# A hybrid SSD and Fourier block: dt cut into steps between gate products, and the order of the last projection pairs

## The chip, the cores and the metric

One NeuronCore of a Trainium2 chip runs the whole program. The metric is the time of one execution on the device, in microseconds (us); the median of several executions counts. All times of the trace are us from the start of the span.

## What is computed

One layer: an input projection of 1024 latent tokens and 256 context tokens, a bidirectional state-space scan (SSD) beside a Fourier mixer, gates, an output projection and a SwiGLU FFN. The part that the change touches is the step size dt of the scan and what is made of it, and the projection columns around it:

```python
u = h @ w_in[i]                                     # x, B, C, dt, z, fft, gate columns
uc = hc @ w_in[i][:, :SSD_IN_WIDTH]
xbc = jax.nn.silu(dwconv_centred(u[..., :CONV_DIM], conv_w, conv_b))
dt_l = jax.nn.softplus(dtr[:, :, d] + bias)
a = -jnp.exp(a_log[d])
a_cum = jnp.cumsum((dt * a), axis=2)                # within chunks of 128
decay_to_end = jnp.exp(a_cum[:, :, -1:] - a_cum)
chunk_decay = jnp.exp(a_cum[:, :, -1])
lmat = decay_matrix(a_cum)                          # exp of differences, lower triangle
y_off = jnp.einsum('bclgn,bcgjpn,bclgj->bclgjp', cc, entering, jnp.exp(a_cum))
gates = jax.nn.sigmoid(u_gate)
```

## The kernel before

All matrices are float32, held as a high and a low part (`hi`, `lo`), so that a product is three matmuls. In the projection stage two blocks of 128 columns are made together by `pair`: it splits two weight tiles and forms seven products p1 to p7 of 512 x 512 (a Strassen-like scheme), each of 12 matmuls, with the input's sums `hT1` to `hT4` prepared beforehand; `combine` (lines 566 to 576) adds them into two padded rows `pads[0]` and `pads[1]`. The order of the products is p1, p2, p4, p6, p3, p7, p5 (another one for the first pair). Behind each product but the first, `trs()` takes one entry of the list `tr` and runs it.

`block_pair(b)` is a pair of x, B or C columns. Its `emit` runs `a_conv` on both pads: a copy with scale on ScalarE (line 429), four multiply-adds on VectorE (line 432), Silu (line 434), and a store for B and C. The result lies in a tile named `cv`, of which there are two in turn. Up to b = 24 its list `tr` transposes the two blocks before. `gate_pair(j)` is a pair of gate columns: `combine`, tanh in the pads (line 683) and a store to `s_gate` from the pads. In what follows x22 is `block_pair(22)` and g0 is `gate_pair(0)`.

The list `steps` is x2 to x22, then g0, x24, g2, x26, g4, x28, g6, x30, g8. `dt_product` has made the raw dt earlier and left it in `s_dt`. After step 14 (x26) `phase_dt` runs whole: it loads dT into a `cv` tile, turns it by ten transposes (line 614) and keeps u and e in a second `cv` tile; softplus is a reciprocal and a polynomial (lines 621 to 633); two matmuls with triangles cumulate (line 641), two more pick the chunk ends (line 646), ScalarE makes `decp` by 18 small exponentials (line 651) and `ea_all`; eight transposes and 16 writes bring the cumulated rows to `s_a` from a third `cv` tile `ar` (line 663); a fourth, `dc`, serves the logarithm (lines 670 to 675). At the end a loop restores `hB12` from `s_q` (lines 718 to 721), whose place hT4 had taken.

PSUM in this stage: pool `ppm` has three banks, pool `ppa` two banks `tr` and three banks `mm`. `a_ps` counts its calls in `nmm` and takes a bank of `ppa` where the count is odd, of `ppm` where it is even. The scan stage behind it takes the banks of `ppm` for its fill products (`fill_ps`) and those of `ppa` for states and outputs; its fill starts with z columns, whose results `zs` lie where the pads were. `NGP = 5` gate pairs are made in the projection stage, the gate blocks 10 to 14 in the scan stage.

In this stage no order is written out by hand. The program gives the instructions in an order, and a scheduler with a timing model lays them on each engine's queue as their inputs become ready in its model. On the chip each engine runs its queue in order.

Of the kernel before, what the change touches and what calls it, by code (L numbers as in the profile page):

```python
# [9 lines left out]
F32 = mybir.dt.float32  # L10
F32R = mybir.dt.float32r
AF = mybir.ActivationFunctionType
ALU = mybir.AluOpType
# [128 lines left out]
def _build(nc, tc, h, o, hook, stop, es):  # L142
# [357 lines left out]
    def pair(src, tr, ctx, emit, late=False):  # L500
# [102 lines left out]
        nc.scalar.copy(out=dT[:, 1024:1280], in_=pss[2][:64, :LC])  # L603
        nc.sync.dma_start(out=s_dt, in_=dT[:, :1280])

    def phase_dt():
        dT = pa.tile([P, 1282], F32, name="cv", bufs=2)[:64]
        nc.sync.dma_start(out=dT[:, :1280], in_=s_dt)
        ue = pa.tile([P, 1282], F32, name="cv", bufs=2)
        u = ue[:, :640].rearrange("p (a b) -> p a b", b=64)  # L610
        for q0 in (0, 5):
# [5 lines left out]
        uf = u.rearrange("p a b -> p (a b)")  # L617
        e = ue[:, 640:1280]
        r = pq = a_all.rearrange("p a b -> p (a b)")
        acc = wst_all.rearrange("p a b -> p (a b)")  # L620
        nc.vector.scalar_tensor_tensor(out=e, in0=uf, scalar=-1.0, in1=uf, op0=ALU.mult, op1=ALU.min)
        nc.scalar.activation(out=e, in_=e, func=AF.Exp)
        nc.vector.tensor_scalar(out=r, in0=e, scalar1=2.0, scalar2=None, op0=ALU.add)
        nc.vector.reciprocal(out=r, in_=r)
        nc.vector.scalar_tensor_tensor(out=e, in0=e, scalar=2.0, in1=r, op0=ALU.mult, op1=ALU.mult)
        nc.vector.tensor_tensor(out=pq, in0=e, in1=e, op=ALU.mult)
        cf = [1.0 / ((2 * k + 1) * 4.0 ** k) for k in range(9)]
        nc.vector.tensor_scalar(out=acc, in0=pq, scalar1=cf[8], scalar2=None, op0=ALU.mult)
        for k in range(7, 0, -1):
            nc.vector.scalar_tensor_tensor(out=acc, in0=acc, scalar=cf[k], in1=pq, op0=ALU.add, op1=ALU.mult)  # L630
        nc.vector.scalar_tensor_tensor(out=acc, in0=acc, scalar=1.0, in1=e, op0=ALU.add, op1=ALU.mult)
        dtf = dt_all.rearrange("p a b -> p (a b)")
        nc.vector.scalar_tensor_tensor(out=dtf, in0=uf, scalar=0.0, in1=acc, op0=ALU.max, op1=ALU.add)
        ae = rows[:, 64:128]
        nc.scalar.activation(out=ae, in_=ae, func=AF.Exp)
        da = e.rearrange("p (a b) -> p a b", b=64)
        nc.vector.scalar_tensor_tensor(out=da, in0=dt_all, scalar=-1.0, in1=ae[:, None, :].to_broadcast([P, NTA, 64]),
                                       op0=ALU.mult, op1=ALU.mult)
        for d, tri in ((0, tri_f), (1, tri_b)):
            ps = ppa.tile([P, 512], F32, name="tr", bufs=2)  # L640
            nc.tensor.matmul(ps[:, :320], lhsT=tri, rhs=da[:, :, 32 * d:32 * d + 32], start=True, stop=True)
            nc.scalar.copy(out=a_all[:, :, 32 * d:32 * d + 32], in_=ps[:, :320].rearrange("p (a b) -> p a b", b=32))
        ex = acc.rearrange("p (a b) -> p a b", b=64)
        for d, sel in ((0, e127), (1, e0)):
            ps = ppa.tile([P, 512], F32, name="tr", bufs=2)
            nc.tensor.matmul(ps[:, :320], lhsT=sel, rhs=a_all[:, :, 32 * d:32 * d + 32], start=True, stop=True)
            psv = ps[:, :320].rearrange("p (a b) -> p a b", b=32)
            nc.vector.tensor_tensor(out=ex[:, :, 32 * d:32 * d + 32], in0=psv, in1=a_all[:, :, 32 * d:32 * d + 32], op=ALU.subtract)
            order = [8, 9, 0, 1, 2, 3, 4, 5, 6] if d == 0 else [9, 8, 7, 6, 5, 4, 3, 2, 1]
            for i, c_ in enumerate(order):  # L650
                nc.scalar.activation(out=decp[:, i, d, :], in_=psv[:, c_, :], func=AF.Exp)
        nc.scalar.activation(out=ex, in_=ex, func=AF.Exp)
        nc.vector.tensor_tensor(out=wst_all, in0=dt_all, in1=ex, op=ALU.mult)
        nc.scalar.activation(out=ea_all, in_=a_all[:, :NT, :], func=AF.Exp)
        ar = pa.tile([P, 1282], F32, name="cv", bufs=2)[:64, :1024].rearrange("p (a b) -> p a b", b=P)
        for q0 in (0, 4):
# [4 lines left out]
        for d in range(2):  # L661
            for g in range(NG):
                nc.sync.dma_start(out=s_a[g, :, d].rearrange("c j l -> j c l"),
                                  in_=ar[32 * d + 4 * g:32 * d + 4 * g + 4])


        lg, cl = u[:, :NT, :], dt_all[:, :NT, :]
        el = e[:, :NT * 64].rearrange("p (a b) -> p a b", b=64)
        dc = pa.tile([P, 1282], F32, name="cv", bufs=2)[:, :NT * 64].rearrange("p (a b) -> p a b", b=64)
        nc.vector.tensor_scalar(out=dc, in0=cl, scalar1=1.2e-38, scalar2=None, op0=ALU.max)  # L670
        nc.scalar.activation(out=lg, in_=dc, func=AF.Ln)
        nc.scalar.activation(out=el, in_=lg, func=AF.Exp, scale=-1.0)
        nc.vector.tensor_tensor(out=el, in0=el, in1=dc, op=ALU.mult)
        nc.vector.scalar_tensor_tensor(out=lg, in0=el, scalar=-1.0, in1=lg, op0=ALU.add, op1=ALU.add)
        nc.vector.tensor_tensor(out=a_all[:, :NT, :], in0=lg, in1=a_all[:, :NT, :], op=ALU.subtract)
        nc.vector.tensor_tensor(out=tri_b, in0=tri_b, in1=ident, op=ALU.subtract)

    def gate_pair(j):
# [38 lines left out]
    for i in range(4):  # L717
        for q in range(2):
            t = small()
            nc.sync.dma_start(out=t, in_=s_q[2 * i + q])  # L720
            nc.vector.tensor_copy(out=hB12[i][q], in_=t)
    hstack_t.close()
    phA.close()
    if hook is not None:
        for nm, t in (("dt_all", dt_all), ("a_all", a_all), ("wst_all", wst_all), ("ea_all", ea_all), ("decp", decp)):
            hook(nm, t)
    if stop == "A":
        right.close(); hstack.close()
# [931 lines left out]
```

## Time and profile before

| | us |
|---|---|
| median of 3 runs | 2282.3 |
| lowest and highest | 2280.68, 2285.83 |
| the profiled execution | 2281.2 |
| its span, first to last instruction | 2279.4 |
| TensorE busy in the span | 2165.9 (95%) |
| VectorE busy | 1627.0 (71%) |
| ScalarE busy | 991.4 (43%) |
| GpSimd busy | 741.8 (33%) |

The page of the profile gives busy time per engine, the span in 40 slices, and the costliest groups of instructions. PE is TensorE, PEld its weight loads, DVE VectorE, ACT ScalarE, POOL GpSimd, SP the engine that issues the transfers. A view by stretches gives busy time of each engine between two times, the count of records in brackets, and the granted TensorE clock as a share of 2.4 GHz. A timeline gives start, duration, engine, line, operation and tiles of each instruction, and in square brackets the idle time before it with what ended it. A list of waits adds up who waited for whom.

### The profile page before, as it was taken

To read this page: it belongs to the slowest core of one execution; us is meant where nothing else is said; L and a number is where in the kernel's file an instruction comes from. 1 tells how busy PE (TensorE), PEld (TensorE's weight loads), DVE (VectorE), ACT (ScalarE), POOL (GpSimd) and SP (SyncE) were. 2 spreads that over 40 slices of the span, in tenths; PEclk is the share of its full clock that TensorE was granted. 3 is DMA by queue.
4 is the path that set the end of the run, shared out by engine and by line. 5 is a ranking of instruction groups with operands and counts; after the bars stand their busy time and mean duration, and the time that the engine had idled before them with its cause. 6 is when DMAs were issued, how large, how long until landed. Compare 5 with 4: busy or idle time off the path is not lost. (4 is left out here: it accounts for less than half of the span.)

```text
span 2279.4 us, 32757 instructions
## 1 busy us (share of the span) xinstructions
PE 2165.9 (95%) x11560; PEld 1813.0 (80%) x11560; DVE 1627.0 (71%) x2783; ACT 991.4 (43%) x2094; POOL 741.8 (33%) x610
## 2 busy tenths in 40 slices
PE   7999999999689999999999999999798999999997
PEld 1778888886588999999989887777576888887876
DVE  5878888888657777877736558826987566775678
ACT  4444444433345666767743212124422332334443
POOL 1532111110125555555521222135343333332222
PEclk9999999999799999999999999999899999999999
DMA  8122223432254555555454546551486224457755
GB/s 289 64 73 88 83 84 130 143 119 93 90 171 152 176 160 171 173 175 178 156 188 164 177 159 245 186 187 65 127 276 226 92 98 162 166 177 242 237 194 185
DMA packets 167101, 360.28 MB, mean 158 GB/s; under 512 B 17548, under 2 KB 57228, under 8 KB 166296
## 3 DMA queue, kind: packets, MB, share of 16 engines
q1 hardware_dynamic: 166936, 358.18, 47.0%
q8 instruction: 91, 1.49, 0.3%
q14 instruction: 74, 0.61, 0.1%
HBM read 267.34 MB, written 90.78 MB: 157 GB/s over the span
## 5 line engine op out<-in xcount | busy, mean ns | idle before, releaser
L199 POOL TENSOR_TENSOR wlo<-wraw,whi 128x1024 fp32r<-128x1024 f32 (+1 forms) x83 | 201.5, 2431 | 634.3 <-ACT whi L198 631.5
L198 ACT CAST whi<-wraw 128x1024 fp32r<-128x1024 f32 (+1 forms) x123 | 126.8, 1036 | 237.6 <-PE dm L210 84.2
L203 PE MATMUL fill<-whi,hhi 128*128 128x256 f32 x768 | 223.1, 292 | 7.1 <-DVE pad L576 5.8
L432 DVE SCALAR_TENSOR_TENSOR cv<-pad,vecs,cv 128x1282 f32<-128x1282 f32 (+1 forms) x128 | 213.8, 1709 | 7.8 <-ACT cv L429 7.4
L204 PE MATMUL fill<-wlo,hhi 128*128 128x256 f32 x768 | 218.1, 284 | 0.0
L205 PE MATMUL fill<-whi,hlo 128*128 128x256 f32 x768 | 217.4, 284 | 0.0
L874 ACT ACTIVATE abc<-abc,a_all 128x128 f32<-128x128 f32 x512 | 158.2, 392 | 88.4 <-DMA abc<-s_a 84.1
L203 PE MATMUL fp<-m,oph 128*128 128x512 f32 x452 | 181.3, 402 | 14.0 <-ACT oph L1343 10.4
L205 PE MATMUL fp<-m,opl 128*128 128x512 f32 x452 | 181.7, 403 | 8.0 <-DVE opl L1344 5.0
L204 PE MATMUL fp<-m,oph 128*128 128x512 f32 x452 | 181.2, 401 | 0.0
L495 PE MATMUL mm<-tq,whi 128*128 128x512 f32 x480 | 153.8, 401 | 1.4 <-ACT whi L198 1.4
L203 PEld LDWEIGHTS fill<-whi,hhi 128*128 128x128 f32 x768 | 145.8, 190 | 9.4 <-issue 6.2
L495 PE MATMUL mm<-hhi,whi 128*128 128x512 f32 x320 | 127.7, 400 | 22.4 <-DVE pad L570 22.4
L204 PEld LDWEIGHTS fill<-wlo,hhi 128*128 128x128 f32 x768 | 146.3, 191 | 0.7
L205 PEld LDWEIGHTS fill<-whi,hlo 128*128 128x128 f32 x768 | 146.0, 190 | 0.5
L495 PE MATMUL mm<-hlo,whi 128*128 128x512 f32 x320 | 127.1, 397 | 0.0
L495 PE MATMUL mm<-hhi,wlo 128*128 128x512 f32 x320 | 126.9, 397 | 0.0
L203 PEld LDWEIGHTS fp<-m,oph 128*128 128x128 f32 x452 | 86.5, 191 | 36.1 <-ACT oph L1343 11.7
L205 PEld LDWEIGHTS fp<-m,opl 128*128 128x128 f32 x452 | 86.3, 191 | 32.0 <-DVE opl L1344 7.6
L495 PEld LDWEIGHTS mm<-tq,whi 128*128 128x128 f32 x480 | 89.7, 189 | 22.7 <-ACT whi L198 2.5
L850 DVE SCALAR_TENSOR_TENSOR S<-S,decp,st 128x64 f32<-128x64 f32 x512 | 105.0, 273 | 0.0
L876 DVE COPY_PREDICATED abc<-misc,abc 128x512 f32<-128x512 int32 x64 | 52.3, 818 | 71.2 <-ACT abc L874 71.1
(408 smaller groups left out, 5919.0 us busy)
## 6 DMA issues: line engine op xcount, KB each, us to landing
abc<-s_a SPq DMA_DIRECT2D x64, 512.0 KB
fraw<-in_wfi SPq DMA_DIRECT2D x44, 512.0 KB
wraw<-in_wxbc SPq DMA_DIRECT2D x32, 512.0 KB
dx<-in_wada SPq DMA_DIRECT2D x32, 512.0 KB
wraw<-in_wzf SPq DMA_DIRECT2D x24, 512.0 KB
gt<-s_gate SPq DMA_DIRECT2D x24, 512.0 KB
fi<-in_wfo SPq DMA_DIRECT2D x22, 512.0 KB
s_cw<-fo SPq DMA_DIRECT2D x44, 256.0 KB
```

Of the source, the lines that this page charges most:

```text
L198: nc.scalar.copy(out=hi[:, :cols], in_=raw[:, :cols])
L199: (eng or nc.gpsimd).tensor_tensor(out=lo[:, :cols], in0=raw[:, :cols], in1=hi[:, :cols].bitcast(F32), op=ALU.subtract)
L203: nc.tensor.matmul(ps, lhsT=a[0], rhs=b[0], start=start, stop=False)
L204: nc.tensor.matmul(ps, lhsT=a[0], rhs=b[1], start=False, stop=False)
L205: nc.tensor.matmul(ps, lhsT=a[1], rhs=b[0], start=False, stop=stop)
L432: nc.vector.scalar_tensor_tensor(out=v[:, :n], in0=pd[:, t:t + n], scalar=cwh[:, 5 * b + t:5 * b + t + 1], in1=v[:, :n], op0=ALU.mult, op1 ...
L495: nc.tensor.matmul(ps, lhsT=lhs[x], rhs=b[i][y], start=i == 0 and (x, y) == (0, 0), stop=i == 3 and (x, y) == (1, 0))
L850: nc.vector.scalar_tensor_tensor(out=sn[:, hd_], in0=S[-1][:, hd_], scalar=decp[:, i, d, 4 * g + j:4 * g + j + 1], in1=sv_[:, hd_], op0=AL ...
L874: nc.scalar.activation(out=abc[:, d, j, :], in_=abc[:, d, j, :], func=AF.Identity, scale=-1.0, bias=a_all[:, c, hd:hd + 1])
L876: nc.vector.copy_predicated(out=E, mask=tri_b.bitcast(mybir.dt.int32)[:, None, :].to_broadcast([P, HPG, P]), data=abc[:, 1])
```

## The change

It does three things. `phase_dt` becomes `dt_steps`, which returns lists of short functions; each list is given to a gate pair as its `tr` list, so that `trs()` runs one function behind each product but the first. g0 gets the load, the transposes and the softplus down to the first polynomial steps, g2 the rest of it, the cumulation, the exponentials and the writes of `s_a`, g4 the logarithm; g6 gets nothing, and g8 gets the four restores of `hB12` behind two empty functions. The tiles change: u lies in `dt_all`, e in the tile that later holds `ea_all` and `decp`; a `cv` tile serves dT, one serves `ar`, and two serve the logarithm. Each gate pair now stands behind its x pair: x22, x24, g0, x26, g2, x28, g4, x30, g6, g8. And before g8 the count `nmm` is made even, so its p1 takes a bank of `ppa`, p2 one of `ppm`, and so on. The 18 exponentials into `decp` become three. The gate blocks of the scan stage stay.

```diff
-    NGP, DTP = 5, 14
+    NGP = 5
...
-    ea_all = dpool.tile([P, NT, 64], F32, name="ea_all")
-    decp = dpool.tile([P, 9, 2, 32], F32, name="decp")
+    ead = dpool.tile([P, NT * 64 + 9 * 64], F32, name="ead")
+    ea_all = ead[:, :NT * 64].rearrange("p (a b) -> p a b", b=64)
+    decp = ead[:, NT * 64:].rearrange("p (a b c) -> p a b c", b=2, c=32)
...
         def trs(n=1):
             for _ in range(n):
                 if tr:
-                    a_transposes(*tr.pop(0))
+                    f = tr.pop(0)
+                    f() if callable(f) else a_transposes(*f)
...
-    def phase_dt():
+    def dt_steps():
+        u = dt_all
+        e = ead[:, :640]
+        r = pq = a_all.rearrange("p a b -> p (a b)")
+        acc = wst_all.rearrange("p a b -> p (a b)")
...
+        def load():
+            dT = keep["dT"] = pa.tile([P, 1282], F32, name="cv", bufs=2)[:64]
+            nc.sync.dma_start(out=dT[:, :1280], in_=s_dt)
+            nc.scalar.activation(out=ae, in_=ae, func=AF.Exp)
+
+        def turn(q0):
+            tp = ppa.tile([P, 512], F32, name="tr", bufs=2)
...
+        def soft_a():
+            stt(out=e, in0=uf, scalar=-1.0, in1=uf, op0=ALU.mult, op1=ALU.min)
+            nc.scalar.activation(out=e, in_=e, func=AF.Exp)
+            nc.vector.tensor_scalar(out=r, in0=e, scalar1=2.0, scalar2=None, op0=ALU.add)
+            nc.vector.reciprocal(out=r, in_=r)
...
+        def cumulate():
+            for d, tri in ((0, tri_f), (1, tri_b)):
...
+        def ends(d):
...
-                nc.scalar.activation(out=decp[:, i, d, :], in_=psv[:, c_, :], func=AF.Exp)
+            if d == 0:
+                nc.scalar.activation(out=decp[:, 0:2, 0, :], in_=psv[:, 8:10, :], func=AF.Exp)
+                nc.scalar.activation(out=decp[:, 2:9, 0, :], in_=psv[:, 0:7, :], func=AF.Exp)
+            else:
+                nc.scalar.activation(out=decp[:, :, 1, :], in_=psv[:, 9:0:-1, :], func=AF.Exp)
...
+        def log_a():
+            le = pa.tile([P, 1282], F32, name="cv", bufs=2)
+            dc = keep["dc"] = pa.tile([P, 1282], F32, name="cv", bufs=2)[:, :NT * 64].rearrange("p (a b) -> p a b", b=64)
...
+        return [[load, both(turn, 0, 5), soft_a, soft_b, part(poly, 7), part(poly, 5)],
+                [lambda: (poly(3), poly(1)), soft_c, cumulate, both(ends, 0, 1), weights, both(rows_out, 0, 4)],
+                [log_a, log_b]]
...
-        pair([h["wgate"][j], h["wgate"][j + 1]], [], False, emit)
+        pair([h["wgate"][j], h["wgate"][j + 1]], tr, False, emit)
...
-        steps += [("g", 2 * i), ("x", 24 + 2 * i)]
+        steps += [("x", 24 + 2 * i), ("g", 2 * i)]
     steps += [("g", 8)]
+    def restore(i):
+        for q in range(2):
+            t = small()
+            nc.sync.dma_start(out=t, in_=s_q[2 * i + q])
+            nc.vector.tensor_copy(out=hB12[i][q], in_=t)
+    rest = [lambda i=i: restore(i) for i in range(4)]
+    nothing = lambda: None
+    later = dt_steps() + [[], [nothing, nothing] + rest]
     for i, (kd, b) in enumerate(steps):
         if kd == "x":
             block_pair(b)
         else:
-            gate_pair(b)
-        if i == DTP:
-            phase_dt()
-    for i in range(4):
-        for q in range(2):
...
+            if b == 8:
+                nmm[0] += nmm[0] % 2
+            gate_pair(b, later.pop(0))
```

## Rows read from the trace of the kernel before

**Rows 1.** The page, part 2: TensorE's busy tenths in 40 slices

```profile
PE   7999999999689999999999999999798999999997
```

**Rows 2.** Stretches: busy us (records) of PE, PEld, DVE, ACT, POOL; clock; DMA

```profile
418.50:440.00 21.50, 21.50 (x102) 17.56 (x101) 21.12 (x18) 10.84 (x14) 2.44 (x1) 1.00 0.36 123
480.00:500.00 20.00, 20.00 (x88) 16.09 (x87) 12.48 (x18) 6.17 (x7) 2.40 (x1) 1.00 0.35 113
500.00:520.00 20.00, 20.00 (x87) 16.14 (x86) 19.66 (x21) 8.54 (x9) 3.00 (x1) 1.00 0.29 105
...
562.60:590.26 27.66, 2.58 (x12) 1.19 (x10) 15.57 (x20) 12.94 (x30) 0.00 (x0) 0.57 0.10 29
590.26:611.50 21.24, 21.24 (x84) 17.07 (x85) 12.08 (x17) 6.27 (x7) 2.40 (x1) 0.92 0.32 124
611.50:631.27 19.77, 19.76 (x85) 15.61 (x83) 19.57 (x21) 7.10 (x8) 6.47 (x2) 1.00 0.43 133
631.27:637.07 5.80, 0.00 (x1) 0.03 (x1) 5.51 (x8) 3.75 (x4) 2.36 (x1) 0.79 0.67 182
```

**Rows 3.** Waits of PE from 540 to 660: total us, times, longest us

```profile
PE mm L495 <- DVE pad L570: 22.4, 1, 22.4
PE fill L203 <- DVE pad L576: 5.8, 1, 5.8
PE tr L659 <- ACT decp L651: 2.0, 1, 2.0
PE mm L495 <- ACT whi L198: 0.9, 1, 0.9
PE tr L659 <- ACT cv L660: 0.7, 1, 0.7
```

**Rows 4.** Timeline of DVE, 554 to 590: start, duration, instruction [idle before <-releaser]

```profile
554.02 0.82 DVE L637 SCALAR_TENSOR_TENSOR cv<-dt_all,rows 128x640 f32<-128x640 f32 x1
...
575.84 0.43 DVE L670 TENSOR_SCALAR cv<-dt_all 128x512 f32<-128x512 f32 x1 [6.83 <-DMA s_a<-cv]
...
581.03 8.58 DVE L432 SCALAR_TENSOR_TENSOR cv<-pad,vecs,cv 128x1024 f32<-128x1024 f32 x7
589.52 0.69 DVE L570 TENSOR_TENSOR pad<-cu,mm 128x512 f32<-128x512 f32 x1
```

**Rows 5.** Timeline of the SP queue: the writes of s_a

```profile
568.65 5.59 SPq L663 DMA_DIRECT2D s_a<-cv  x16
```

**Rows 6.** Timeline of ACT: a function table load, the function behind it, the first zs

```profile
576.94 1.28 ACT L672 ACT_TABLE_LOAD   x1
578.24 0.63 ACT L672 ACTIVATE cv<-cv 128x512 f32<-128x512 f32 x1
...
642.87 0.39 ACT L761 ACTIVATE zs<-fill 128x256 f32<-128x256 f32 x1 [4.50 <-DMA s_gate<-pad]
```

**Rows 7.** Groups of DVE by line, 518 to 592: count | busy us, mean ns

```profile
L630 DVE SCALAR_TENSOR_TENSOR wst_all<-wst_all,a_all 128x640 f32<-128x640 f32 x7 | 5.8, 824 | 0.1
L624 DVE RECIPROCAL a_all<-a_all 128x640 f32<-128x640 f32 x1 | 4.2, 4153 | 0.0
...
L615 DVE TENSOR_TENSOR cv<-tr,rows 128x320 f32<-128x320 f32 x2 | 0.9, 486 | 0.0
```

**Rows 8.** Timeline of PE: a pair's start, the old turn, the fill's start, the first state product

```profile
500.21 0.40 PE L495 MATMUL mm<-hhi,whi 128*128 128x512 f32 x1
...
525.04 0.83 PE L614 MATMUL tr<-misc,cv 64*128 64x64 f32 x10
...
637.07 0.55 PE L203 MATMUL fill<-whi,hhi 128*128 128x256 f32 x1 [5.81 <-DVE pad L576]
...
641.57 0.28 PE L203 MATMUL fill<-whi,hhi 128*128 128x256 f32 x1
...
648.52 0.59 PE L840 MATMUL st<-xwf,bh 128*128 128x256 f32 x2
```

**Rows 9.** Timeline of POOL: the first state operand

```profile
644.77 1.19 POOL L833 TENSOR_TENSOR xwb<-xh,wst_all 128x256 f32<-128x256 f32 x2 [7.84 <-DMA xh<-s_x]
```

More of the change, by code (lines that the diff above doesn't have):

```diff
@@ L604, in dt_product @@
         nc.sync.dma_start(out=s_dt, in_=dT[:, :1280])
-    def phase_dt():
[L607 to L611, printed above, removed]
+    def dt_steps():
+        u = dt_all
+        uf = u.rearrange("p a b -> p (a b)")
+        e = ead[:, :640]
+        r = pq = a_all.rearrange("p a b -> p (a b)")
+        acc = wst_all.rearrange("p a b -> p (a b)")
+        ex = acc.rearrange("p (a b) -> p a b", b=64)
+        da = e.rearrange("p (a b) -> p a b", b=64)
+        ae = rows[:, 64:128]
+        cf = [1.0 / ((2 * k + 1) * 4.0 ** k) for k in range(9)]
+        stt = nc.vector.scalar_tensor_tensor
+        keep = {}
+        def load():
[3 more added lines that the diff above has]
+        def turn(q0):
+            dT = keep["dT"]
             tp = ppa.tile([P, 512], F32, name="tr", bufs=2)
@@ L616, in phase_dt @@
                                     in1=rows[:, None, 0:64].to_broadcast([P, 5, 64]), op=ALU.add)
[L617 to L638, printed above, removed]
@@ L639, in phase_dt @@
-        for d, tri in ((0, tri_f), (1, tri_b)):
-            ps = ppa.tile([P, 512], F32, name="tr", bufs=2)
[L641 to L646, printed above, removed]
+        def soft_a():
[3 more added lines that the diff above has]
+            nc.vector.reciprocal(out=r, in_=r)
@@ new lines, in soft_b, with poly, soft_c @@
+        def soft_b():
+            stt(out=e, in0=e, scalar=2.0, in1=r, op0=ALU.mult, op1=ALU.mult)
+            nc.vector.tensor_tensor(out=pq, in0=e, in1=e, op=ALU.mult)
+            nc.vector.tensor_scalar(out=acc, in0=pq, scalar1=cf[8], scalar2=None, op0=ALU.mult)
+        def poly(k0):
+            for k in (k0, k0 - 1):
+                if k > 0:
+                    stt(out=acc, in0=acc, scalar=cf[k], in1=pq, op0=ALU.add, op1=ALU.mult)
+        def soft_c():
+            stt(out=acc, in0=acc, scalar=1.0, in1=e, op0=ALU.add, op1=ALU.mult)
+            stt(out=uf, in0=uf, scalar=0.0, in1=acc, op0=ALU.max, op1=ALU.add)
+            stt(out=da, in0=dt_all, scalar=-1.0, in1=ae[:, None, :].to_broadcast([P, NTA, 64]), op0=ALU.mult, op1=ALU.mult)
@@ new lines, in cumulate @@
+        def cumulate():
+            for d, tri in ((0, tri_f), (1, tri_b)):
+                ps = ppa.tile([P, 512], F32, name="tr", bufs=2)
+                nc.tensor.matmul(ps[:, :320], lhsT=tri, rhs=da[:, :, 32 * d:32 * d + 32], start=True, stop=True)
+                nc.scalar.copy(out=a_all[:, :, 32 * d:32 * d + 32], in_=ps[:, :320].rearrange("p (a b) -> p a b", b=32))
+        def ends(d):
+            ps = ppa.tile([P, 512], F32, name="tr", bufs=2)
+            nc.tensor.matmul(ps[:, :320], lhsT=(e127, e0)[d], rhs=a_all[:, :, 32 * d:32 * d + 32], start=True, stop=True)
@@ L654, in phase_dt @@
-        nc.scalar.activation(out=ea_all, in_=a_all[:, :NT, :], func=AF.Exp)
-        ar = pa.tile([P, 1282], F32, name="cv", bufs=2)[:64, :1024].rearrange("p (a b) -> p a b", b=P)
-        for q0 in (0, 4):
+            if d == 0:
[3 more added lines that the diff above has]
+                nc.scalar.activation(out=decp[:, :, 1, :], in_=psv[:, 9:0:-1, :], func=AF.Exp)
@@ L657, in phase_dt, with weights, rows_out @@
+        def weights():
+            nc.scalar.activation(out=ex, in_=ex, func=AF.Exp)
+            nc.vector.tensor_tensor(out=wst_all, in0=dt_all, in1=ex, op=ALU.mult)
+            nc.scalar.activation(out=ea_all, in_=a_all[:, :NT, :], func=AF.Exp)
+        def rows_out(q0):
+            if q0 == 0:
+                keep["ar"] = pa.tile([P, 1282], F32, name="cv", bufs=2)[:64, :1024].rearrange("p (a b) -> p a b", b=P)
+            ar = keep["ar"]
             tp = ppa.tile([P, 4, P], F32, name="tr", bufs=2)
@@ L660, in phase_dt @@
             nc.scalar.activation(out=ar[:, q0:q0 + 4, :], in_=tp[:64], func=AF.Copy, scale=-1.0)
[L661 to L676, printed above, removed]
@@ L678, in gate_pair @@
-    def gate_pair(j):
+            if q0 == 4:
+                for d in range(2):
+                    for g in range(NG):
+                        nc.sync.dma_start(out=s_a[g, :, d].rearrange("c j l -> j c l"),
+                                          in_=ar[32 * d + 4 * g:32 * d + 4 * g + 4])
+        def log_a():
+            le = pa.tile([P, 1282], F32, name="cv", bufs=2)
+            keep["lg"], keep["el"] = [le[:, 512 * q:512 * q + 512].rearrange("p (a b) -> p a b", b=64) for q in range(2)]
+            dc = keep["dc"] = pa.tile([P, 1282], F32, name="cv", bufs=2)[:, :NT * 64].rearrange("p (a b) -> p a b", b=64)
+            nc.vector.tensor_scalar(out=dc, in0=dt_all[:, :NT, :], scalar1=1.2e-38, scalar2=None, op0=ALU.max)
+            nc.scalar.activation(out=keep["lg"], in_=dc, func=AF.Ln)
+            nc.scalar.activation(out=keep["el"], in_=keep["lg"], func=AF.Exp, scale=-1.0)
@@ new lines, in log_b @@
+        def log_b():
+            lg, el = keep["lg"], keep["el"]
+            nc.vector.tensor_tensor(out=el, in0=el, in1=keep["dc"], op=ALU.mult)
+            stt(out=lg, in0=el, scalar=-1.0, in1=lg, op0=ALU.add, op1=ALU.add)
+            nc.vector.tensor_tensor(out=a_all[:, :NT, :], in0=lg, in1=a_all[:, :NT, :], op=ALU.subtract)
+            nc.vector.tensor_tensor(out=tri_b, in0=tri_b, in1=ident, op=ALU.subtract)
+        part = lambda f, *a: (lambda: f(*a))
+        both = lambda f, x, y: (lambda: (f(x), f(y)))
@@ L724, in _build @@
     if hook is not None:
-        for nm, t in (("dt_all", dt_all), ("a_all", a_all), ("wst_all", wst_all), ("ea_all", ea_all), ("decp", decp)):
+        for nm, t in (("dt_all", dt_all), ("a_all", a_all), ("wst_all", wst_all), ("ead", ead)):
             hook(nm, t)
```

8 lines of the change are left out of this document (1 added, 7 removed).

## The prediction

> **What bounds the kernel now.** I read the page's slices first: TensorE is at nine tenths or more nearly everywhere, so the time is TensorE's stream plus its holes, and a hole shows as a digit under nine. Slices 10 and 11 (counted from zero, 570 to 684 us) are such a place, a 6 and an 8 [rows 1]. Then the table of stretches: from 562.60 to 590.26 TensorE works 2.58 of 27.66 us, and from 631.27 to 637.07 not at all [rows 2]. The list of TensorE's waits between 540 and 660 us names the causes: 22.4 us for line 570 of VectorE, 5.8 us for line 576, and 3.6 us in three short ones, 31.8 us in all [rows 3].
>
> The first hole is not VectorE's load but its order. Line 570 is the first addition of a pair's results; it writes a pad. The timeline of VectorE shows what stands before it: line 670 waits 6.83 us for the writes of s_a to leave a cv tile, the logarithm and exponential on ScalarE and three additions follow, then comes a whole convolution (7 steps, 8.58 us), and only then line 570 at 589.52 [rows 4]. So the chain is: all of dt holds tiles of the two-deep cv ring; the convolution of x28 gets no cv tile until dt's last part is through; the pads are not free until that convolution has read them; gate pair 6 can't be added up; its PSUM banks stay full; pair x30 can't start. The 16 writes of s_a are issued in 5.59 us [rows 5].
>
> The second hole is at the border of the stages. The scan stage's fill products take the three banks of pool ppm. By the parity of a_ps the last pair (gate 8) has p1, p4, p3, p5 there, and line 576, which reads p4, is the last of the seven additions.
>
> Both holes leave TensorE at its lower level (1.2 GHz, granted 0.57 and 0.79 in them) for a while after: the pair after the first takes 21.24 us, where 84 matmuls at the pace of the pair before the border (85 in 19.77) are 19.5, so 1.7 us lost [rows 2]. After the second the matmuls come every 0.214 us between 637.07 and 641.57 (21 intervals) and every 0.118 us later (59 from there to the first st product at 648.52), so 21 x 0.096 = 2.0 us lost [rows 8].
>
> **The change part by part.** *dt in steps.* In the new order (x22, x24, g0, x26, g2, x28, g4, x30, g6, g8) dt takes one cv tile in g0, one (ar) in g2 and two in g4, each between the convolutions and no longer all before that of x28. The hole goes: 27.66 less TensorE's own 2.58, which stays, is 25.1, with the clock 26.8 us. No matmul is added. Three of the steps put matmuls between products (turn, cumulate with ends, rows_out).
>
> *What is late next: VectorE.* A pair lasts 19.5 us on TensorE. In the window behind an x pair VectorE does that pair's convolution and is busy 19.66 of 20 us; behind a gate pair it is busy 12.48 of 20 [rows 2]. List 0 costs 2 x 0.49 (line 615), 4.15 (reciprocal), four steps of line 630 at 0.82, three others of 640 columns at 0.82 and two at 0.49: 11.9 us. List 1 costs six of 0.82, two of 0.49 and one of 0.83: 6.7 us; list 2 (three of 512 columns, two shorter) about 2.8, all by the pace of [rows 7]. List 0 can't begin in g0's first half: dT needs a cv tile, so the convolution of x24 and its store come first. Before, dT was turned at 525.04, some 25 us after x26, the pair whose convolution it had to wait for, had ended (the next pair's first product stands at 500.21) [rows 8]. So list 0 falls into x26's window, list 1 into g2's: 12.5 + 11.9 + 19.7 + 6.7 = 50.8 us of VectorE in two windows of 19.5, an excess of 11.8. x28's window has 7 free to take it up, if the dt steps give way to convolution and weight splits. Bounds of what TensorE pays: nothing (they give way; the scheduler orders by readiness, and before it let dt and splits alternate at a cost of one 0.9 us wait [rows 3]), or 11.8 (they go first) plus 1.7 for the clock. Less than nothing is excluded, since no work leaves VectorE. I take 5, nearer to the first because of that 0.9 us row. One more place: the second convolution of x28 needs ar's tile, so the s_a writes; by the old pace (line 637 ends at 554.84, line 670's wait at 575.84, 21 us [rows 4]) that is just in time. Bounds nothing and the old 6.83; I take 1. Together 6.
>
> *x24 straight behind x22.* Behind x22, with its longer convolution, VectorE was busy 21.12 of 21.50 us while TensorE had no hole [rows 2]; x24 adds its transposes to TensorE's side, so its cover is longer than that of g0, which stood there. Nothing; if the cover is gone, the excess is below 1 us.
>
> *Queues passed.* SP: dT's load and the 16 writes (5.59 us of issue) now stand ahead of weight loads of x26 and g4. Weights are loaded two tiles ahead, with several microseconds to spare before their products; nothing, or at most those 5.59 if a load stood right behind. POOL: no instruction of dt is on it. ScalarE: 18 small exponentials become 3 wide ones, a saving off the path. Its function table changes more often, since Silu of the convolutions now comes between the lists; one load is 1.28 us and the next function starts at once [rows 6]. I count three more, 3.8 us on an engine that is busy less than half the time: nothing on TensorE.
>
> The Trainium skill (ScalarE: Activation LUTs, What ACT_TABLE_LOAD costs) speaks against such interleaving: it gives a switch 2.66 us, since a drain follows the load. The trace disagrees here, load and next function are back to back; by the page the three switches would be 8.0 us on ScalarE, and still beside TensorE.
>
> *The last pair's banks and the restore.* With nmm made even, ppm holds p2, p6, p7, read by lines 570 to 572; p7 is finished one product before the end, and no convolution stands in front, as g6 precedes g8. So the fill can start when the last product ends: 5.8 + 2.0 = 7.8 us. What is late next: the first zs waits until 642.87 for the gate's store to leave the pads, and the first state product needs xh (xwb at 644.77) [rows 6, 9]. Both hang on the pair's last additions, which move earlier by about 3.5 us, not by 5.8; the state product, which stood at 648.52, would be there before its operand by some 2 us. So 5.5 of 7.8 stay. Bounds: 0 (weights or xh late) and 7.8. The restore (8 casts of about 0.4 us and 8 loads) moves into g8's window, where VectorE is free: nothing.
>
> **Sum** against the profiled execution (2281.2 us, span 2279.4): 2281.2 - 26.8 - 5.5 + 6 = 2254.9. The median of the runs is 2282.3, 1.1 above; I keep 2255. The scan and FFN stages are not touched; TensorE is full there, so a shift passes through.
>
> **Rivals.** (1) *Everything hidden*: dt gives way everywhere and the border loses its whole hole: 2281.2 - 26.8 - 7.8 = 2246.6. For it: the 0.9 us row; against: two windows over-full. (2) *VectorE becomes the bound*: the steps go before convolution and splits, TensorE pays 11.8, 1.7 for the clock, some 3 more at g4, and the border gives 5.5: 2281.2 - 26.8 - 5.5 + 16.5 = 2265.4. For it: a saturated g window [rows 2]; against: readiness, not list order, sets the queue. (3) *TensorE waits in its own queue, and it is slower*: matmuls go in order, so a dt matmul in front of a product holds it up. If the scheduler sets turn where the code has it, after three of g0's products (8.4 us in) while dT comes some 25 us after the pair's start, that is 16 us; cumulate and ends in g2 8; rows_out 2.7 as in [rows 3]; clock 3 x 1.7; with the 6 of above 38, against a gain of 32.3: 2287. It decides from about 32 us of such waits. Against it: the old turn stood at 525.04 with no wait before it [rows 8]. (4) *It doesn't do what it says*: dt bunches up again and x28's convolution still stands behind it; only the 6.83 us of waiting and the border go, 2281.2 - 6.8 - 5.5 = 2269, or with the old hole kept whole 2276 to 2282. Against: ar and the log tiles are now allocated on either side of x28.
>
> **How the numbers follow.** Forecast (2248 to 2262) 0.53; (1) 0.15; (2) 0.16; (3) 0.09; (4) 0.07. A measurement of this kernel tells about 0.2% (4.6 us) from no change. Faster takes the forecast, (1), (2) and half of (4): 0.87; within 0.2%: the rest of (4) and the mild part of (3): 0.05; slower 0.08. The range runs from below (1) to above (2), 2245 to 2270, which leaves out (3) and part of (4).
>
> **What would show it.** Right: no wait of TensorE over 10 us between 540 and 640; line 670's counterpart without a wait for s_a; the first fill product within 2 us of the last mm product; more table loads; short waits for the first addition (line 570's counterpart) at the ends of g0, g2 or g4, 6 us in all. Wrong: a TensorE wait on dT, da or a_all (rival 3), or a VectorE queue in which dt steps stand in a row before a convolution (rival 2), or a new late hole where xh comes in.

## The result, and the profile after

The changed kernel takes **2254.9 us** (median of 4 runs, 2250.87 to 2256.37) against 2282.8 for the kernel before on the same chip: ratio 0.9874, 95% interval 0.9857 to 0.9891. The profiled execution took 2255.2 us, with a span of 2253.5. A second series of runs of the same pair gave 2254.3 and 2282.7, ratio 0.9877 (0.9859 to 0.9896).

The slices of the page, TensorE's row: where [rows 1] had a 6 and an 8, there are nines.

```profile
PE   7999999999999999999999999998898999999997
```

All of TensorE's waits between 400 and 660 us (total, times, longest). In place of five waits of together 31.8 us, the longest 22.4 and 5.8 [rows 3], stand 3.4, 1.8 and 0.6, together 5.8. The last of them lies behind the first fill product.

```profile
PE mm L496 <- DVE pad L572: 3.4, 1, 3.4
PE mm L496 <- ACT whi L198: 1.8, 1, 1.8
PE fill L204 <- POOL wlo L199: 0.6, 1, 0.6
```

TensorE's timeline (start, duration, instruction): the first transposes within x22, the two products that wait, the first fill product, the first state product. The fill now starts 0.23 us after the last mm product, without a wait and at the full clock (0.28 us for a product that took 0.55 in [rows 8]).

```profile
414.47 1.04 PE L421 MATMUL tr<-misc,cv 128*128 128x128 f32 x8
...
506.40 0.77 PE L496 MATMUL mm<-hhi,whi 128*128 128x512 f32 x1 [3.41 <-DVE pad L572]
...
561.71 0.73 PE L496 MATMUL mm<-tq,whi 128*128 128x512 f32 x2 [1.84 <-ACT whi L198]
...
612.22 0.28 PE L203 MATMUL fill<-whi,hhi 128*128 128x256 f32 x1
...
624.25 0.67 PE L881 MATMUL st<-xwf,bh 128*128 128x256 f32 x2
```

**A measure that doesn't drift.** The stage begins a few microseconds earlier or later from one execution to the next (the same transposes stand at 412.78 in the trace before and at 409.75 in the second profile of the changed kernel), so absolute times can't be subtracted. I cut each trace at three marks which all the kernels have: those first transposes in x22, the first fill product, and the first em product (the start of the FFN stage). For the kernel before the first mark is this row:

```profile
412.78 1.04 PE L420 MATMUL tr<-misc,cv 128*128 128x128 f32 x8
```

The table gives the three lengths in us: the **section** (x22's transposes to the fill; before 637.07 - 412.78 = 224.29), the scan stage (fill to em) and the rest (em to the end of the span). Only the section holds code that the change touches. The lengths are those of one profiled execution of each kernel, the ratios those of all its executions.

| kernel | section | fill to em | em to end | ratio of whole time (95%) |
|---|---|---|---|---|
| before | 224.3 | 841.1 | 801.2 | 1 |
| after | 197.8 | 843.1 | 798.2 | 0.9874 (0.9857, 0.9891) |
| after, second series | 197.8 | 841.9 | 799.4 | 0.9877 (0.9859, 0.9896) |
| before + even banks (e2) | 220.9 | 843.1 | 796.6 | 1.0005 (0.9996, 1.0015) |
| before + new order (e3) | 219.4 | 846.6 | 789.2 | 0.9953 (0.9931, 0.9974) |
| before + dc in PSUM (e5) | 217.0 | 838.9 | 798.5 | 0.9976 (0.9965, 0.9987) |
| after, dt in one lump (e6) | 218.4 | 843.4 | 798.0 | 0.9990 (0.9979, 1.0000) |
| after, old banks (e1) | 199.9 | 845.7 | 798.7 | 0.9925 (0.9910, 0.9940) |
| after + 2 reciprocals (e7) | 207.5 | 854.4 | 797.2 | 0.9961 (0.9947, 0.9974) |
| after, lists in x pairs (e8) | 199.5 | 842.2 | 796.9 | 0.9898 (0.9883, 0.9912) |
| after, second list in x28 (e11) | 197.6 | 845.6 | 798.1 | 0.9864 (0.9845, 0.9882) |
| after, TensorE in code order (e9) | 213.6 | 847.8 | 790.2 | 0.9923 (0.9897, 0.9949) |
| after, x28's split moved (e12) | 195.8 | 843.8 | 796.3 | 0.9897 (0.9862, 0.9932) |
| after, g2's split moved (e13) | 199.8 | 843.2 | 788.6 | 0.9848 (0.9830, 0.9866) |

The two profiles of the changed kernel agree to 0.01 us in the section (197.75 and 197.76); the change takes 26.5 us out of it.

### The profile page after: what moved, and what is told of

It reads as the page before. It is cut to its first block, busy times and chain, and to the rows that moved or that the text cites. A ratio compares the mean times of both kernels' runs of the same rounds, so it can differ in the third digit from the quotient of the medians.

```text
span 2253.5 us, 32731 instructions
## 1 busy us (share of the span) xinstructions
PE 2164.4 (96%) x11560; PEld 1809.4 (80%) x11560; DVE 1629.2 (72%) x2783; ACT 991.6 (44%) x2082; POOL 742.0 (33%) x610
## 5 line engine op out<-in xcount | busy, mean ns | idle before, releaser
L891 DVE SCALAR_TENSOR_TENSOR S<-S,ead,st 128x64 f32<-128x64 f32 x512 | 104.7, 271 | 0.0
```

Of the source, the lines that this page charges most:

```text
L891: nc.vector.scalar_tensor_tensor(out=sn[:, hd_], in0=S[-1][:, hd_], scalar=decp[:, i, d, 4 * g + j:4 * g + j + 1], in1=sv_[:, hd_], op0=AL ...
```

## The experiments: the border

**Even banks alone.** In the kernel before:

```diff
+            if b == 8:
+                nmm[0] += nmm[0] % 2
```

> The kernel before, with nothing but the count made even ahead of the last pair. My theory: the border of the stages is held by two things, the banks and the convolution of x30 in front of the last additions. So the long wait for line 570 (22.4 us) stays, and the wait of the first fill product falls only from 5.8 to about 3, since lines 570 to 572 still stand behind the convolution: 2282.8 - 3 = about 2280. Rival: the banks are the whole of the border, the wait goes and the clock stays up: 2275. Rival: the banks do nothing: 2283.

Measured: 0.9996 to 1.0015, section 220.9, 3.4 less than before. TensorE's longest wait, and the fill in the timeline:

```profile
PE mm L495 <- DVE pad L570: 22.3, 1, 22.3
...
633.86 0.36 PE L203 MATMUL fill<-whi,hhi 128*128 128x256 f32 x1 [2.47 <-DVE pad L571]
```

The first hole is untouched and the second goes from 5.8 to 2.5 us: by other banks the fill hangs on line 571 instead of 576, and still on an addition, because in the old order the last x pair's convolution stands in VectorE's queue ahead of these.

**The other way: all of the change, old banks.** The changed kernel without the two lines above:

```diff
-            if b == 8:
-                nmm[0] += nmm[0] % 2
```

> The changed kernel without the even count ahead of the last pair. My theory: p4 lies in a bank of ppm again, so the first fill product waits until the seventh addition has read it, about 2.7 us after the last product, and nothing else changes: 2255 + 3 = 2258. Rival: with no convolution in front of the additions the banks do nothing: 2255, no wait at the fill.

Measured: section 199.9, 2.2 longer than with them. In the timeline the fill waits again, for line 577, the sixth of the seven additions (the seventh was expected):

```profile
614.37 0.36 PE L203 MATMUL fill<-whi,hhi 128*128 128x256 f32 x1 [1.47 <-DVE pad L577]
```

The 2.2 us are near what was expected; the rest of the 5.3 us by which its span is longer than after's (2258.8) lies behind the fill, 845.7 instead of 843.1 and 798.7 instead of 798.2, in stages whose code is the same.

**The new order alone.** In the kernel before, dt still in one piece, behind x26:

```diff
-    NGP, DTP = 5, 14
+    NGP, DTP = 5, 13
...
-        steps += [("g", 2 * i), ("x", 24 + 2 * i)]
+        steps += [("x", 24 + 2 * i), ("g", 2 * i)]
```

> The kernel before, with each x pair ahead of its gate pair; dt whole behind x26 as it was, its tiles and banks as they were. My theory: dt's four tiles of the cv ring still stand between the convolutions of x26 and x28, so the wait of TensorE for the first addition stays at 15 to 25 us; the border loses the convolution in front of the last additions, some 3 us: about 2279. Rival: the order of the pairs is what brings the gain: 2256 to 2262, no wait over 8 us.

Measured: by the list of TensorE's waits the hole stays, and the border's wait falls to 1.5 us with the old banks:

```profile
PE mm L495 <- DVE pad L570: 23.4, 1, 23.4
PE fill L203 <- DVE pad L575: 1.5, 1, 1.5
```

The section gains 4.9 us, although the hole is a microsecond longer. The banks alone gained 3.4, and in the changed kernel they are worth 2.2. So both act on the same wait, and the order (two gate pairs at the end, no convolution ahead of the last additions) does somewhat more. By the medians the whole kernel is 8.3 us faster than before on the same chip (2269.3 against 2277.6; ratio 0.9953), where some 3 were expected; the table shows where: its last part takes 789.2 instead of 801.2 us. More on that below.

## The experiments: the hole

**Everything but the steps.** The changed kernel with its tiles, order and banks, and all the steps run in one lump behind x26:

```diff
-    later = dt_steps() + [[], [nothing, nothing] + rest]
+    lump = [f for part_ in dt_steps() for f in part_]
+    later = [[], [], [], [], [nothing, nothing] + rest]
...
+            if b == 26:
+                for f in lump:
+                    f()
```

> The changed kernel, with the same steps run one behind the other behind x26 and not between products; tiles, order of pairs and banks as changed. My theory (dt must take its cv tiles between different convolutions): the ring holds up x28's convolution again, a wait of 15 to 22 us for the first addition is back, the border stays short: 2255 + 18 = about 2273. Rival (new tiles, order and banks bring the gain): 2255, no wait over 6 us.

TensorE's longest wait in it:

```profile
PE mm L496 <- DVE pad L572: 24.0, 1, 24.0
```

Measured: the hole is back, section 218.4. Against before this leaves 5.9 us for order and banks together, against after 20.6 us for spreading the steps. x28's convolution stands behind the lump again, whose logarithm waits 8.0 us on ScalarE for the writes of s_a. The new tiles and the leaner code of dt itself (three wide exponentials for 18) don't shorten the hole: 24.0 us here, 23.4 with the old code in the same order (e3).

**Is it the ring?** In the kernel before, one tile of dt's last part is taken from PSUM instead of the cv ring, so line 670 need not wait for the writes of s_a:

```diff
-        dc = pa.tile([P, 1282], F32, name="cv", bufs=2)[:, :NT * 64].rearrange("p (a b) -> p a b", b=64)
+        dc = ppa.tile([P, 512], F32, name="tr", bufs=2).rearrange("p (a b) -> p a b", b=64)
```

> The kernel before, with the tile dc of the logarithm in a PSUM bank and no longer in the cv ring. My theory (VectorE stands behind the ring, in order): the wait for the writes of s_a (6.83 us) goes, the chain to the first addition is shorter by about that, and the wait of TensorE falls from 22.4 to about 16: 2276. Rival (VectorE's load is the bound): the wait stays near 22 and the time near 2282.

TensorE's two long waits in it:

```profile
PE mm L495 <- DVE pad L570: 15.7, 1, 15.7
PE fill L203 <- DVE pad L576: 5.8, 1, 5.8
```

Measured: 22.4 becomes 15.7, by 6.7 us, as much as line 670 had waited (6.83 [rows 4]); section 7.3 shorter. So the wait for the ring passed through to TensorE whole. The other 15.7 us are put down to the rest of the chain, dt's queue and a convolution behind it, by the rows alone: taking all of dt off the ring wasn't tried.

**Is what is left VectorE's load?** The changed kernel with its reciprocal computed three times over (1/(1/(1/x)) leaves the value as it is), 8.3 us more of VectorE:

```diff
-            nc.vector.reciprocal(out=r, in_=r)
+            for _ in range(3):
+                nc.vector.reciprocal(out=r, in_=r)
```

> The changed kernel with two more reciprocals on VectorE in the first list (2 x 4.15 = 8.3 us; inverting three times leaves the value). My theory: the 3.4 us that TensorE still waits at the end of g2 come from VectorE's excess in the windows of x26 and g2; 8.3 us more go mostly into that wait, which becomes 8 to 12 us: 2261 to 2264. Rival: the dt steps give way and the wait has another cause: it stays near 3.4, 2255.

Measured: section 207.5, so 8.3 us of VectorE cost 9.8 us. They aren't in one wait, and the whole time, 2270.4, lies above both expectations. Two stretches (busy us and records of PE, PEld, DVE, ACT, POOL; clock; DMA) show VectorE full for 40 us and a lower clock, and under them stand the two largest entries in the list of TensorE's waits, the first of them made of 3.0 us at 509 and 3.3 us at 597:

```profile
480.00:500.00 20.00, 15.88 (x60) 11.62 (x60) 20.00 (x22) 4.85 (x5) 0.00 (x0) 0.91 0.09 29
500.00:520.00 20.00, 17.00 (x66) 13.22 (x65) 19.97 (x25) 9.29 (x10) 2.69 (x1) 0.91 0.29 112
...
PE mm L496 <- DVE pad L572: 6.3, 2, 3.3
PE mm L496 <- ACT whi L198: 2.9, 1, 2.9
```

TensorE's waits from 400 to 660 come to 11.8 us with those not shown, 6.0 more than after (0.9 and 0.6 of the two sums lie behind the fill); the granted clock, 0.91, 0.91, 0.90 and 0.93 in the four disturbed stretches of 20 us, would cost some 7.0 us (20 x 0.35) against 3.4 for the one stretch at 0.83 below (20 x 0.17). That is an estimate; with the waits it makes 9.6. No slack is left on VectorE here: this work cost TensorE its full length and the clock on top.

The same stretches of the changed kernel: VectorE full in the first, TensorE short of work in the second.

```profile
480.00:500.00 20.00, 20.00 (x87) 16.12 (x86) 20.00 (x24) 7.50 (x8) 2.39 (x1) 1.00 0.16 53
500.00:520.00 20.00, 16.59 (x60) 12.81 (x59) 18.32 (x25) 8.54 (x11) 0.00 (x0) 0.83 0.33 124
```

**The lists elsewhere.** First all three lists of steps one pair later, between the products of x26, x28 and x30:

```diff
-    later = dt_steps() + [[], [nothing, nothing] + rest]
+    later = [[], [], [], [], [nothing, nothing] + rest]
+    in_x = dict(zip((26, 28, 30), dt_steps()))
...
+            block_pair(b, in_x.get(b, ()))
```

> The changed kernel with the three lists one pair later, behind the products of x26, x28 and x30, whose windows leave VectorE some 7 us each. My theory: the convolution of x26 no longer has list 1 beside it, the 3.4 us at the end of g2 go: 2251 to 2253. Rival: dt now ends later, the convolutions of x28 and x30 wait for their cv tiles, and a wait of 5 to 15 us is back at g4 or g6: 2260 to 2270.

TensorE's two largest waits in it, from 400 to 660:

```profile
PE mm L496 <- DVE wlo L199: 3.1, 2, 1.7
PE mm L496 <- DVE pad L572: 2.4, 1, 2.4
```

A miss: the wait for line 572 shrinks to 2.4, others come, and the section is 1.7 us longer. Then only the second list one pair later (x28 for g2), the third in x30:

```diff
-    later = dt_steps() + [[], [nothing, nothing] + rest]
+    l0, l1, l2 = dt_steps()
+    later = [l0, [], [], [], [nothing, nothing] + rest]
+    in_x = {28: l1, 30: l2}
...
+            block_pair(b, in_x.get(b, ()))
```

> The changed kernel with the first list of dt steps kept between the products of g0, the second list moved from g2 to the pair behind it, x28, and the third from g4 to x30. If the 3.4 us wait at the end of g2 stands there because VectorE has g2's additions and the second list at once, it goes or falls under 1.5 us, no other wait over 2 us comes, and the fill starts 2 to 4 us earlier (608 to 610 instead of 612.2). If VectorE is simply short of time over the whole stretch from x26 to x28, or the convolutions of x28 now wait behind the ar tile in the ring, the wait turns up in x28 or x30 and the fill starts at 612 to 615. Whole time by the first 2251 to 2253, by the second 2254 to 2260.

The product that waits, in TensorE's timeline:

```profile
501.58 0.77 PE L496 MATMUL mm<-hhi,whi 128*128 128x512 f32 x1 [3.40 <-DVE pad L572]
```

Measured: the same wait at the same place (91.93 us behind x22's transposes, 506.40 - 414.47 in after) and a section of 197.6 us. Neither expectation came true, and the run didn't test the second list: from x22's transposes until 18 us behind this wait VectorE's queue holds the same instructions in the same order as in after. The first two steps of the second list stand ahead of the wait in both, because the scheduler places them where their inputs are ready, not where the program gives them. What part the list has in the wait stays open. The changed kernel itself beside it:

> The changed kernel itself, beside the one above on the same chip. The same waits as in its first profile (3.4 us at the end of g2, 1.8 and 0.6 behind it), fill at 612, 2252 to 2257.

It repeats its waits (3.4, 1.9, 0.6) and its section; 2254.3 and 2251.9 us can't be told apart by their intervals.

**What the 3.4 us are made of.** VectorE's timeline of the changed kernel ahead of that wait; between the rows stand x26's additions, splits of weights and six steps of dt's polynomial (line 649), four of list 0 and the first two of list 1:

```profile
474.08 4.15 DVE L639 RECIPROCAL a_all<-a_all 128x640 f32<-128x640 f32 x1
...
491.11 2.47 DVE L433 SCALAR_TENSOR_TENSOR cv<-pad,vecs,cv 128x1024 f32<-128x1024 f32 x2
...
495.37 4.63 DVE L433 SCALAR_TENSOR_TENSOR cv<-pad,vecs,cv 128x1024 f32<-128x1024 f32 x2
499.92 0.81 DVE L649 SCALAR_TENSOR_TENSOR wst_all<-wst_all,a_all 128x640 f32<-128x640 f32 x1
...
505.58 0.67 DVE L572 TENSOR_TENSOR pad<-cu,mm 128x512 f32<-128x512 f32 x1
```

GpSimd's timeline in the same time:

```profile
475.64 2.40 POOL L199 TENSOR_TENSOR wlo<-wraw,whi 128x1024 fp32r<-128x1024 f32 x1 [19.10 <-ACT whi L198]
495.33 2.39 POOL L199 TENSOR_TENSOR wlo<-wraw,whi 128x1024 fp32r<-128x1024 f32 x1 [17.29 <-ACT whi L198]
```

Two steps of x26's convolution take 4.63 us where two others take 2.47, and beside them runs GpSimd's split of x28's first weights. Both engines read SBUF there. Two runs put that to the test: the split of one pair goes to VectorE, where it costs 1.22 us, once the one beside the long steps (x28's) and once the one beside the reciprocal (g2's). The first of the two edits:

```diff
...
-        w0 = wsplit(raw[0])
+        w0 = wsplit(raw[0], eng=eng0)
...
+        pair([h["wxbc"][b], h["wxbc"][b + 1]], tr, ctx, emit, b == 2, nc.vector if b == 28 else None)
```

> The changed kernel with the first weight split of x28 on VectorE instead of GpSimd, 1.22 us more of VectorE's own work in the window behind x26; nothing else changes. In the changed kernel this GpSimd split (495.33, 2.39 us) runs beside a step of x26's convolution, and two steps take 4.63 us there instead of 2.47. If the two engines hold each other up, VectorE saves 2.16 and pays 1.22: the 3.4 us wait of TensorE at x28's start becomes about 2.5 and the fill stands about 1 us earlier against the transposes of x22 (196.8 instead of 197.75). If the long step has another cause, VectorE only gets 1.22 more: wait 4.6, section 199. Whole time 2252 to 2256 either way.

The two steps in VectorE's timeline, and the product that waits:

```profile
495.49 2.48 DVE L433 SCALAR_TENSOR_TENSOR cv<-pad,vecs,cv 128x1024 f32<-128x1024 f32 x2
...
501.24 0.77 PE L496 MATMUL mm<-hhi,whi 128*128 128x512 f32 x1 [2.71 <-DVE pad L572]
```

> The same edit for the first weight split of g2 alone (475.64 in the changed kernel), which runs beside the reciprocal, 4.15 us there as elsewhere. By the theory that GpSimd delays only those steps of VectorE that read two operands from SBUF, nothing is saved here and 1.22 us is added: wait at x28's start 4.6, section 199 instead of 197.75. If every GpSimd split costs VectorE something, the wait stays near 3.4 or falls. Whole time 2254 to 2258 either way.

The same rows of this kernel:

```profile
497.59 4.62 DVE L433 SCALAR_TENSOR_TENSOR cv<-pad,vecs,cv 128x1024 f32<-128x1024 f32 x2
...
505.48 0.76 PE L496 MATMUL mm<-hhi,whi 128*128 128x512 f32 x1 [3.81 <-DVE pad L572]
```

Measured: with x28's split on VectorE no steps are long any more, the wait is 2.7 and the section 195.8, two microseconds shorter although VectorE got more work to do. About one was expected. TensorE's wait is only 0.7 us shorter; the larger part is the clock behind it, by an estimate from the starts of the products: 15 products in 6.21 us behind the wait in after, 2.7 us more than at their later pace of 0.233 us, and here 9 in 3.63 us, 1.5 us more. With g2's split moved the long steps stay, the wait is 3.8 and the section 199.8, two longer. The split beside the reciprocal had cost nothing, the one beside the convolution 2.2 us of VectorE. (By its whole time the second of these is the fastest kernel of all, 2245.9 us; the table shows that in the last part, 788.6 us.)

**TensorE in the order of the code.** Rival 3 of the prediction, made real: from the pair before g0 to g4 TensorE's queue is kept as the code has it.

```diff
+        with (tc.manual_schedule(engines={mybir.EngineType.PE}) if 11 <= i <= 16 else ExitStack()):
```

> The changed kernel with TensorE's queue in the order of the code from x24 to g4, so that turn, cumulate, ends and rows_out stand exactly between the products where trs() has them. It prices rival 3. If that rival's mechanism is real: TensorE waits some 16 us for dT at turn in g0 and some 10 us in g2, in all 20 to 30 us: 2275 to 2287. If it is not: the waits are below 5 us and the time stays near 2257.

TensorE's two longest waits from 400 to 660:

```profile
PE tr L631 <- DMA cv<-s_dt: 13.9, 1, 13.9
PE tr L421 <- ACT cv L435: 3.8, 1, 3.8
```

Measured: the wait at turn is 13.9 us (the prediction had priced it at 16), but cumulate, ends and rows_out wait for nothing, where it had 10.7. The section is 15.9 us longer than after, and still 10.7 shorter than before. The whole time, 2261.7, fits neither expectation: the last part, 790.2 us, is 8 us shorter than after's.

## Why the prediction came out right

*The bound and the mechanism.* Right. The lump shows that the hole is made by dt in one piece, and the PSUM tile that the ring's wait went through to TensorE to the microsecond. The signs listed are there: no wait over 10 us, the fill within 0.23 us of the last mm product, short waits of 5.8 us in all where 6 were expected, the largest for the first addition at the end of g2. That the sums agree is in part luck: only 3.4 us are waits for a first addition, and the 1.8 us come from ScalarE, where nothing was expected.

*First hole less VectorE's excess, 26.8 - 6 = 20.8 us.* Measured by the lump against after: 218.36 - 197.75 = 20.6. The two terms can't be parted by these runs. Read from after's trace, what is left is larger than 6: waits of 3.4 and 1.8 us and the 2.7 us of clock behind the first, 7.9 by that estimate. The 5 of the 11.8 was a choice between bounds, and its reason, that dt steps give way, is only half true: dt's steps did go between x26's convolution steps, and by the run with x28's split moved 2.0 us of the section are GpSimd's doing, which the prediction hadn't seen at all ("POOL: no instruction of dt is on it" was true and not enough).

*The ar and log tiles, 1 us, and ScalarE, nothing.* Line 670's counterpart doesn't wait for s_a; it waits a little for the store of a convolution's tile. In VectorE's timeline:

```profile
546.32 1.22 DVE L697 TENSOR_SCALAR cv<-dt_all 128x512 f32<-128x512 f32 x1 [1.33 <-DMA s_cT<-cv]
```

On ScalarE the logarithm waits 2.71 us for the other tile's store, and then come its table load, the load for tanh, g4's tanh and the exponential, without a gap. Only behind them, at 560.62, stand the casts of the next weights, and TensorE waits 1.84 us for the first of these at 561.71:

```profile
554.48 1.28 ACT L698 ACT_TABLE_LOAD   x1 [2.71 <-DMA s_cT<-cv]
555.77 0.63 ACT L698 ACTIVATE cv<-cv 128x512 f32<-128x512 f32 x1
...
556.90 1.28 ACT L719 ACT_TABLE_LOAD   x1
...
560.62 1.98 ACT L198 CAST whi<-wraw 128x1024 fp32r<-128x1024 f32 x2
```

So "nothing on TensorE" for ScalarE's queue and its loads fell short by up to 1.8 us, and the tile ring has a part in it. In e11 a cast stands ahead of the logarithm's load, and this wait is not there; no run parts the loads from the ring.

*The border, 5.5 us.* For the 5.8 us at the fill, before against the lump gives 5.9, though their other waits differ a little too (24.0 against 22.4 in the hole, 1.3 against 3.6 in the short ones). From the fill to the first state product the prediction had 2.0 less for the clock and 2.3 more for the operands, 0.3 in all: 624.25 - 612.22 = 12.03 against 11.45 in [rows 8], 0.6 more. What is late next is what it named, the gate's store and xh, in the timelines of ScalarE and VectorE:

```profile
619.70 0.66 ACT L802 ACTIVATE zs<-fill 128x256 f32<-128x256 f32 x2 [3.35 <-DMA s_gate<-pad]
...
623.72 1.18 DVE L873 TENSOR_TENSOR xwf<-xh,wst_all 128x256 f32<-128x256 f32 x2 [2.05 <-DMA xh<-s_x]
```

It led with the banks and named the order (g6 ahead of g8) beside them; alone the order gives 4.9 us and the banks 3.4.

*Together* 26.3 us were predicted up to the first state product; from x22's transposes it came 25.96 us earlier (209.78 against 235.74).

*Table loads.* Seven in the stage instead of four, three more as counted, and each next function at once, 0.01 us behind the load. The drain that the Trainium skill counts (ScalarE: Activation LUTs, What ACT_TABLE_LOAD costs) is not seen here either: 554.48 and 1.28 us make 555.76, and the function starts at 555.77.

*"The scan and FFN stages are not touched; a shift passes through."* The weakest step, which did no harm by luck. In after the parts behind the fill moved by +2.0 and -3.0 us and nearly cancel. Over the kernels of the table the time from the fill to the end went from 1631.9 (e13) to 1651.7 us (e7), with the same code there in all. Two causes can be told apart by the order in which the instructions stand on the engines' queues in the traces.

The FFN part has two layouts. In e3, e9 and e13 the queues behind the first em product are the same on all four engines, and 113 of VectorE's 767 instructions stand at another place in them than in after; all other kernels of the table have after's order but for a handful of instructions. The three take 788.6 to 790.2 us for this part, the others 796.3 to 801.2. So the scheduler lays out a later queue anew when something ahead of it moves, and the same code runs in another order. Which step of the scheduling decides between the layouts stays open. Here is the stretch of 80 us that begins 240 us behind em in after, where TensorE is short of work, and the largest difference in the lists of waits from em to the end:

```profile
1695.00:1775.00 80.00, 73.49 (x309) 57.55 (x310) 59.54 (x77) 25.06 (x45) 31.12 (x21) 1.00 0.50 170
...
PE fp L205 <- DVE opl L1385: 6.7, 6, 2.7
```

The same of e13 (columns as above), where TensorE is busy 78.95 us and that wait is 1.1:

```profile
1696.00:1776.00 80.00, 78.95 (x338) 62.90 (x337) 56.19 (x77) 25.80 (x47) 31.74 (x22) 1.00 0.54 180
...
PE fp L205 <- DVE opl L1385: 1.1, 1, 1.1
```

That is 5.5 of the 9.6 us by which e13's last part is shorter.

In the scan stage the order is not all. e11 has the queues of after there, instruction for instruction, and takes 845.6 us where the two profiles of after take 843.1 and 841.9. So a few microseconds go from one execution to the next. The 854.4 of e7 are one execution of a kernel whose nine executions lie between 2263.1 and 2277.2 us; their cause stays open.

*The rivals.* VectorE is the bound in a window, but TensorE pays 3.4 us of wait and some 2.7 us of clock for it, where rival 2 had 11.8 and 1.7. Rival 3's mechanism exists and is worth half of its price (15.9 of some 32 us): even made real by force it doesn't turn the change into a loss. Rival 4 is the lump: a total within 0.2% of before.

## What to carry to other kernels

A long side computation that shares a short ring of tiles with the main loop costs its chain of work and waits in one hole; cut into steps with the loop's own allocations between them, it costs only what overfills the engine it runs on (here 20.6 us came back, of some 26.8 that the hole was put at). Price such a move by a stretch between two marks that both traces have, for the whole time also carries what a new layout makes of stages that nobody touched (8 to 10 us here) and a few microseconds from one execution to the next. And look at the queues in the trace before a run is taken as a test: a scheduler can undo an edit of the program's order. When an engine is full in a window, look at what runs beside it as well as at what was put onto it.

## What the runs showed of the hardware that was not expected

VectorE's convolution steps, which have two operands in SBUF, are held up beside a subtraction of GpSimd in SBUF: two of them take 4.63 us beside a split of 2.39, and 2.47 or 2.48 without. Instructions with one SBUF operand don't all fare alike: the reciprocal takes 4.15 us with a split beside it (after) and without (e13), while a cast of the restore takes 2.26 beside one and 0.43 alone. VectorE's timeline in after:

```profile
604.85 0.43 DVE L751 CAST hhi<-sm 128x512 fp32r<-128x512 f32 x1 [1.28 <-DMA sm<-s_q]
605.83 2.26 DVE L751 CAST hlo<-sm 128x512 fp32r<-128x512 f32 x1 [0.55 <-DMA sm<-s_q]
```

GpSimd's at the same time:

```profile
605.40 2.40 POOL L199 TENSOR_TENSOR wlo<-wraw,whi 128x1024 fp32r<-128x1024 f32 x1 [18.30 <-DVE hhi L751]
```

GpSimd is held up as well. This split, which meets VectorE in the middle of x30's convolution, takes 4.46 us:

```profile
582.64 4.46 POOL L199 TENSOR_TENSOR wlo<-wraw,whi 128x1024 fp32r<-128x1024 f32 x1 [12.32 <-DVE cv L433]
```

The same stands in the kernel before, at the border. VectorE's timeline there, beside splits of GpSimd at 621.05 and 627.54:

```profile
622.57 4.64 DVE L432 SCALAR_TENSOR_TENSOR cv<-pad,vecs,cv 128x1024 f32<-128x1024 f32 x2
...
627.80 4.61 DVE L432 SCALAR_TENSOR_TENSOR cv<-pad,vecs,cv 128x1024 f32<-128x1024 f32 x2
```

These are the steps in front of the last pair's additions, some 4.3 us longer together than without a split. So GpSimd may have a large part in the old wait of 5.8 us; no run moved these splits alone.

The Trainium skill (SBUF — State Buffer, Who interferes with whom) says that VectorE and GpSimd share a pair of SBUF ports as a lock held for a whole instruction, taken by two-input instructions and by casts in a two-port mode. The traces agree. The two steps that begin at 495.37, just behind GpSimd's 495.33, end at 500.00, 2.28 us after GpSimd does, about what two steps take alone; the cast ends 0.29 us after it (608.09 against 607.80); and the reciprocal is spared.

A wait of 3.4 us brought the granted clock to 0.83 over the 20 us it lies in; the wait of 1.8 us at 560 left it at 1.00. The length of a wait doesn't settle it: one of 2.4 us in e8 left the clock of its 20 us (500 to 520) at 1.00, and one of 1.7 us with one of 0.2 us behind it in e13 lowered it to 0.91 (560 to 580).
